# An attention phase on one core: one head's weighing moved behind a bank's copy, and the next weights split behind the exponentials and packings

## The chip, the core and the metric

The kernel runs on one core of a Trainium2 chip. The metric is the device time of one execution in microseconds. Five engines of the core matter here, each with its own list of instructions: TensorE (PE in the profile, its weight loads PEld) multiplies matrices into banks of PSUM, VectorE (DVE) and ScalarE (ACT) do the arithmetic around it, GpSimd (POOL) copies a little and issues some transfers, and SyncE's queue (SP) issues the other transfers between memory and SBUF.

## The reference, cut to what matters

The whole is a two-layer model on 512 tokens of width 1024: dilated attention, a feed-forward block, an mLSTM block, a feed-forward block and a last normalization. The change lies in the attention:

```python
proj = (xn @ w_in).reshape(B, S, N_GROUPS, 3, ATTN_HEADS, ATTN_HEAD_DIM)
for g, (window, dilation) in enumerate(((128, 1), (512, 4), (2048, 16))):
    q = apply_partial_rope(proj[:, :, g, 0], positions) * scale
    k = apply_partial_rope(proj[:, :, g, 1], positions)
    v = proj[:, :, g, 2]
    o, lse = dilated_window_attention(q, k, v, window, dilation)
wts = softmax(stack(lses), axis=0)
o = einsum('gbsh,gbshd->bshd', wts, stack(outs))
return o.reshape(B, S, ATTN_WIDTH) @ w_out
```

So there are three groups, and for each of 8 heads of size 128 a query, a key and a value in each group. The first 32 of 128 features of queries and keys are rotated. The softmax weights of the three groups are joined into one weighing of all probabilities.

## The kernel before, in words

**Split products.** Every float32 product is made of three products of rounded numbers. A weight chunk of 128 x 1024 is loaded raw, ScalarE casts it to the high half (L223, `whi`), and VectorE subtracts that from the raw chunk for the low half (L225, `wlo`). `split_chunk` does both. There are three raw buffers and four pairs of halves, so a chunk can be split only when the matmuls of the fourth chunk before it are done, and a raw buffer is free for its next load when its split is done.

**Pairs and groups.** Heads are taken in four pairs, `a0` to `a3` in the profile's names, and for each pair the three groups one after another (`project_pair`). For pairs 1 to 3 the first group is plain: queries (`a2g0q`) and keys (`a2g0k`) take two chunks each, with two PSUM banks each, and `evac` copies each bank out with a VectorE copy (L1001) and packs the rotated features with ScalarE (L1004). The second and third group (`a2g1`, `a2g2`; `qk_unit`) form queries and keys together by a scheme of seven block products, in the order P1, P5, P6, P2, P7, P3, P4, of 24 matmuls each. Their sums of weight blocks are VectorE subtractions (`less`, L880). P1 and P2 go to bank c, P5 and P3 to bank p, P6, P7 and P4 to bank u, which starts as a copy of c (L944). Three banks tagged `acc` serve the plain groups and these. After P2 and P4 the queries are taken out by ScalarE: the rotated features are packed (L906) and the bank copied (L924). After P7 and P3 VectorE adds a kept copy (L932) and ScalarE packs (L906). After P4 comes the rotation (`rope`): a shuffle (L607), two multiplications (L608, L609), an addition (L616), and four ScalarE copies back (L628). In the very last unit the rotation is done in parts, straight into place (L613).

**Attention of a pair.** `scores0` multiplies queries and keys of the first group, and VectorE adds the mask and takes the maximum (L709); `exponentials` turns the maximum into a shift (L747) and ScalarE takes eight exponentials (L752). `scores12` does the same for the other two groups (L733 on TensorE, L736, L757). `joint` exchanges maxima and sums between the groups (one small product on TensorE, L769) and forms the factors (L785 to L793). `weigh(i)` multiplies the probabilities of head i with them: four VectorE instructions at L801 and four at L804. `transposes(i)` turns the result (L810) and stores it to memory (L813), `bring(i)` loads it back in another order (L818), and `values(i)` multiplies with the values (L828, L833); the result is kept by a ScalarE copy (L640).

**The order of the work.** The attention of a pair runs spread over the projections of the next one. `defer(n, fn)` puts a function on a list for n ticks later; `advance` raises the tick after each chunk of the first group and after the second, fourth, sixth and seventh product of the other two, and calls what is due. Ticks 1 to 4 of a pair are its first group, 5 to 8 the second, 9 to 12 the third. `RUN_AT` says when each step of the pair before is due: `scores12` at 1, the list `rest` at (4, 5, 7, 8, 8, 9), `values` at 11 and 12. `project` calls what is due at tick 4 a little early, between the two banks of the last key chunk (`amid`). `SCORES0_AT` puts a pair's own `scores0` at tick 10, after P2 of its third group. A planner then makes the list of each engine out of the traced instructions; it may move an instruction ahead of others where nothing forbids it. `tc.issue_after(ins)` forbids it: what is traced under it comes behind `ins` on the engine of `ins`. `behind(fn, engine=E)` calls `fn` so behind the last instruction traced on E; `run` does it for TensorE. Two variables do it for the splits: the subtractions come behind `ahead_of_splits[0]` on VectorE, the casts behind `ahead_of_casts[0]` on ScalarE.

**Splits ahead.** `Feed` holds the plan of all weight chunks. `pop` hands out the next and tops the store up to `ahead`; after each product but a unit's first it is topped up to `ahead + 1`. From pair 1 on `ahead` is 3.

Of the kernel before, what the change touches and what calls it, by code (L numbers as in the profile page):

```python
# [33 lines left out]
C2 = float(np.float32(np.uint32(np.float32(TWO_PI - C1).view(np.uint32) & 0xFFFFF000).view(np.float32)))  # L34
C3 = float(np.float32(TWO_PI - C1 - C2))
SCORES0_AT = 6
RUN_AT = (1, (4, 5, 7, 8, 8, 9), (11, 12), (2, 3, 1))
LAST_AT = (1, (2,), (), (1, 1, 1))
STACK_AT = (9, 11, 15, 17)
HEAD_AT = ((9, 10, 12), (10, 11, 13), (12, 13, 15), (13, 14, 16), (15, 16, 18), (16, 17, 19), (18, 19, 21),  # L40
# [33 lines left out]
def tile_hybrid_dilated_attn_mlstm(  # L74
# [62 lines left out]
    tick = [0]  # L137
# [4 lines left out]

    def advance():
        tick[0] += 1
        run_deferred(lambda t: t <= tick[0])

    def run_deferred(due=lambda t: True):
        while True:
            ready = sorted((e for e in later if due(e[0])), key=lambda e: e[:2])
            if not ready:  # L150
                return
            later.remove(ready[0])
            ready[0][2]()
# [4 lines left out]
    def last_on(engine):  # L158
        for ins in reversed(nc.cur_bb.bb.instructions):
            if ins.engine == engine:  # L160
                return ins
# [43 lines left out]
    ahead_of_splits = [None]  # L205
# [198 lines left out]
    with ExitStack() as actx:  # L404
# [253 lines left out]
        def attention_pair(pr, qks):  # L658
# [35 lines left out]
            def scores0(q, k):  # L694

                for i in range(2):
                    for b2 in range(2):
                        sp = score_bank(i, "%ss0" % nm)
                        o, parts = 0, []
                        for b in (2 * b2, 2 * b2 + 1):  # L700
                            lo_ = max(b - 1, 0) * P
                            w = (b + 1) * P - lo_
                            nc.tensor.matmul(sp[:, o:o + w], q[:, i, b * P:(b + 1) * P],
                                             k[:, i, lo_:lo_ + w], start=True, stop=True)
                            parts.append((b, o, w))
                            o += w
                        for b, o, w in parts:
                            pb = max(2 * b - 1, 0)
                            nc.vector.tensor_tensor_reduce(  # L709
                                p0[i][:, pb:pb + w // P, :].rearrange("p a b -> p (a b)"),  # L710
                                sp[:, o:o + w], mask_band[:, 2 * P - w:], 1.0, -3e38,
                                op0=ALU.add, op1=ALU.max, accum_out=own[:, 0, 0, i, b:b + 1])
                ahead_of_splits[0] = last_on(DVE)

                def exps():
                    for i in range(2):
                        exponentials(0, i)
                if pr < HEADS // 2 - 1:
                    exps()
                else:  # L720
                    defer(2, lambda: behind(exps, engine=ACT))

# [73 lines left out]
            def weigh(i):  # L796
                cf4 = weight[0]
                for b in range(4):
                    pb = max(2 * b - 1, 0)
                    blk = p0[i][:, pb:2 * b + 1, :].rearrange("p a b -> p (a b)")  # L800
                    nc.vector.tensor_scalar(blk, blk, cf4[:, 0, i, b:b + 1], None, op0=ALU.mult)  # L801
                for c in range(4):
                    blk = p12[i].rearrange("p (g c) k -> p c g k", g=2)[:, c]
                    nc.vector.tensor_scalar(blk, blk, cf4[:, 1, i, c:c + 1], None, op0=ALU.mult)  # L804
# [11 lines left out]
            def bring(i, queue=nc.gpsimd):  # L816
                pt = ap2.tile([P, 4, 15, R], F32, tag="p", name=nm + "pT", bufs=4)
                queue.dma_start(pt.rearrange("p a n i -> p (a n i)"), pts[i].rearrange("b j a x -> (b j) (a x)"))  # L818
                pts[i] = pt
# [18 lines left out]
                else:  # L838
                    out(2 * pr + i, op)

            def first_rest():
                joint()
                weigh(0)
            rest = (first_rest, lambda: transposes(0), lambda: bring(0), lambda: weigh(1), lambda: transposes(1),
                    lambda: bring(1))
            if pr == HEADS // 2 - 1:
                def all_rest():
                    first_rest()
                    ahead_of_splits[0] = last_on(DVE)
                    ahead_of_casts[0] = last_on(ACT)  # L850
                    transposes(0)
                rest = (all_rest,)
# [44 lines left out]
        def qk_unit(pr, g, qk):  # L897
            nm = "a%dg%d" % (pr, g)
            last = pr == HEADS // 2 - 1 and g == 2
            target = {"P1": "c11", "P2": "c11", "P5": "p5", "P3": "p5", "P6": "u", "P7": "u", "P4": "u"}  # L900
            two_m = lambda t: t.rearrange("p (m s) -> p m s", m=2)
            acc = {}
            rot = vu = None

            def pack(q, src):
                nc.scalar.activation(two_m(rot[0][quarter(q)]), src, AF.Copy)  # L906

            def finish(name):
                nonlocal rot, vu
                if name == "P5":  # L910
                    vu = ap.tile([P, 2, SEQ], F32, tag="vu", name=nm + "vu")
                    nc.scalar.activation(vu[:, 0], acc["p5"], AF.Copy)
                    ahead_of_casts[0] = last_on(ACT)
                elif name == "P6":
                    nc.scalar.activation(vu[:, 1], acc["u"], AF.Copy)
                    ahead_of_casts[0] = last_on(ACT)
                elif name in ("P2", "P4"):
                    th = int(name == "P4")
                    src = two_m(acc[target[name]])
                    if th == 0:  # L920
                        t = ap.tile([P, 2, SEQ], F32, tag="rot", name="rot")
                        rot = t[:, 0], t[:, 1]
                    pack(th, src[:R])
                    nc.scalar.activation(halves(qk[0], th), src, AF.Copy)  # L924
                    ahead_of_casts[0] = last_on(ACT)
                    if last and th:
                        rope(qk, rot, False, 1, 2, True)
                elif name in ("P7", "P3"):
                    th = int(name == "P7")
                    out = halves(qk[1], th)  # L930
                    with behind_scores():
                        nc.vector.tensor_tensor(out, two_m(acc[target[name]]), two_m(vu[:, 1 - th]), op=ALU.add)  # L932
                    pack(2 + th, out[:R])
                    if last and th == 0:
                        rope(qk, rot, False, 0, 1, True)
                        rope(qk, rot, False, 2, 4, True)

            for n, name in enumerate(QK_ORDER):
                key = target[name]
                if name in ("P1", "P5"):  # L940
                    acc[key] = acc_tile(nm + key)
                if name == "P5":
                    acc["u"] = acc_tile(nm + "u")
                    nc.scalar.activation(acc["u"], acc["c11"], AF.Copy)  # L944
                    ahead_of_casts[0] = last_on(ACT)
                    feed.fill(feed.ahead + 1)
                whl = feed.pop()
                with fenced():
                    for m in range(2):
                        for k in range(4):  # L950
                            for a, b in SPLITS:
                                if name in ("P1", "P2", "P4"):
                                    x_ = pair[b][k + 4 * (name != "P1")][:, HALF * (name == "P4"):HALF * (1 + (name == "P4"))]
                                else:
                                    x_ = sum_part(name, b, k)
                                nc.tensor.matmul(acc[key][:, m * HALF:(m + 1) * HALF], whl[a][:, k, m * P:(m + 1) * P], x_,
                                                 start=(name in ("P1", "P5") and m == 0 and k == 0 and (a, b) == SPLITS[0]),
                                                 stop=(m == 1 and k == 3 and (a, b) == SPLITS[-1]), skip_group_check=True)
                finish(name)
                if n == 6 and not last:  # L960
                    back = rope(qk, rot, False)
                    if g == 2:
                        back()
                    else:
                        defer(1, lambda: behind(back, engine=ACT))
                if n in (1, 3, 5, 6):
                    advance()
                if n:
                    feed.fill(feed.ahead + 1)

        def project_pair(pr, qks, then=None):
            nm = "a%d" % pr
# [1411 lines left out]
```

## Time and profile before

| | us |
|---|---|
| median of 3 runs | 1394.45 |
| lowest and highest | 1393.76, 1394.7 |
| the profiled execution | 1396.64 |
| its span, first to last instruction | 1394.9 |
| TensorE busy | 1371.6 |
| VectorE busy | 1111.5 |
| ScalarE busy | 779.8 |

The profile is one execution. A row of a timeline begins with the start in us from the span's start and the duration in us; then come engine, line, operation, what is written and what is read (numbers of buffers left out), shape and count; in brackets stand the idle time before it and what ended that. A row of the list of waits gives who waited for whom, then the total in us, how often, and the longest. A row of the table by stage gives the stretch, its length, the busy us of PE, PEld, DVE, ACT and POOL, and last the granted clock of TensorE (1.00 is full), the busy share of the DMA engines and GB/s.

### The profile page before, as it was taken

What the parts mean: (1) busy time and instruction counts of PE and PEld (TensorE: products, weight loads), DVE (VectorE), ACT (ScalarE), POOL (GpSimd) and SP (SyncE); (2) the same over time, 40 slices, a digit from 0 to 9 for tenths busy, and PEclk for the clock granted to TensorE, in tenths of its full rate; (3) what the DMA queues carried; (4) which work ended last, traced back from release to release, by engine and by line L of the source; (5) the groups of instructions that cost most, each with busy time, mean ns of one, the idle gap of its engine ahead of it and who ended that gap; (6) DMA issues with size and microseconds to landing.
All of it is one profiled execution on the core that took longest, in us unless ns stands there. A gap on an engine that the chain in (4) does not pass through costs nothing. (4 is left out here: it accounts for less than half of the span.)

```text
span 1394.9 us, 22560 instructions
## 1 busy us (share of the span) xinstructions
PE 1371.6 (98%) x8740; PEld 1245.1 (89%) x8740; DVE 1111.5 (80%) x1845; ACT 779.8 (56%) x1246; POOL 178.7 (13%) x264
## 2 busy tenths in 40 slices
PE   9999999999999999999999999999999999999997
PEld 7888889898897889999999998897888899999886
DVE  7758769595878289877878898898858988887887
ACT  6556565655555245444567464785535554458854
POOL 3000013122211000000010100123201230001213
PEclk9999999999999999999999999999999999999999
DMA  8534245537275447333352743324334553335963
GB/s 288 183 121 137 81 146 182 174 117 230 81 252 168 150 138 169 102 121 121 106 154 74 172 118 92 91 76 118 95 116 112 145 181 122 122 110 131 198 165 100
DMA packets 140067, 193.81 MB, mean 139 GB/s; under 512 B 8980, under 2 KB 104788, under 8 KB 139960
## 3 DMA queue, kind: packets, MB, share of 16 engines
q1 hardware_dynamic: 119552, 139.81, 31.5%
q0 software_dynamic: 18752, 51.43, 15.6%
q8 instruction: 69, 1.13, 0.3%
q10 hardware_dynamic: 1656, 1.12, 0.2%
q14 instruction: 38, 0.31, 0.1%
HBM read 167.30 MB, written 22.54 MB: 136 GB/s over the span
## 5 line engine op out<-in xcount | busy, mean ns | idle before, releaser
L1687 POOL DMA_DIRECT2D f1T<-in_ffn_w_out_dram x15 | 17.8, 1185 | 208.7 <-DMA f1P_2w_w<-in_ffn_w_out_dram 136.2
L1662 POOL DMA_DIRECT2D f0S<-in_ffn_w_out_dram x10 | 8.7, 874 | 260.7 <-DVE f0hid L1579 173.0
L2219 POOL DMA_DIRECT2D hD<-hB x32 | 21.7, 696 | 68.5 <-DVE hB L2216 68.5
L255 PE MATMUL mo<-n_h,mo_k_l 128*128 128x512 f32 x64 | 25.3, 395 | 0.0
L255 PE MATMUL mo<-n_h,mo_k_h 128*128 128x512 f32 x64 | 25.2, 393 | 0.0
L255 PE MATMUL mo<-n_l,mo_k_h 128*128 128x512 f32 x64 | 25.2, 393 | 0.0
L255 PE MATMUL awo<-ao_h,awo_k_h 128*128 128x512 f32 x64 | 25.2, 393 | 0.0
L255 PE MATMUL mwo<-yo_l,mwo_k_h 128*128 128x512 f32 x64 | 25.1, 393 | 0.0
L255 PE MATMUL mqk<-n_h,mqk_k_h 128*128 128x512 f32 x64 | 25.1, 392 | 0.0
L255 PE MATMUL mqk<-n_l,mqk_k_h 128*128 128x512 f32 x64 | 25.1, 391 | 0.0
L255 PE MATMUL f0j<-n_h,f0j_h 128*128 128x512 f32 x64 | 25.0, 391 | 0.0
L255 PE MATMUL f1j<-n_h,f1j_h 128*128 128x512 f32 x64 | 25.0, 391 | 0.0
L255 PE MATMUL awo<-ao_h,awo_k_l 128*128 128x512 f32 x64 | 25.0, 391 | 0.0
L255 PE MATMUL mwo<-yo_h,mwo_k_l 128*128 128x512 f32 x64 | 25.0, 391 | 0.0
L255 PE MATMUL mqk<-n_h,mqk_k_l 128*128 128x512 f32 x64 | 25.0, 390 | 0.0
L255 PE MATMUL awo<-ao_l,awo_k_h 128*128 128x512 f32 x64 | 25.0, 390 | 0.0
L255 PE MATMUL f1j<-n_h,f1j_l 128*128 128x512 f32 x64 | 24.9, 390 | 0.0
L255 PE MATMUL f0j<-n_h,f0j_l 128*128 128x512 f32 x64 | 24.9, 390 | 0.0
L255 PE MATMUL f0j<-n_l,f0j_h 128*128 128x512 f32 x64 | 24.9, 389 | 0.0
L255 PE MATMUL f1j<-n_l,f1j_h 128*128 128x512 f32 x64 | 24.9, 389 | 0.0
L255 PE MATMUL mwo<-yo_h,mwo_k_h 128*128 128x512 f32 x64 | 24.8, 391 | 0.0
L225 DVE TENSOR_TENSOR v1P_l<-v1W,v1P_h 128x1024 fp32r<-128x1024 f32 x14 | 17.1, 1223 | 9.3 <-ACT v1P_h L223 9.3
(2613 smaller groups left out, 5881.1 us busy)
## 6 DMA issues: line engine op xcount, KB each, us to landing
f0j_w<-in_ffn_w_in_dram SPq DMA_DIRECT2D x17, 512.0 KB, 4.7
f1j_w<-in_ffn_w_in_dram SPq DMA_DIRECT2D x17, 512.0 KB, 6.5
f1T<-in_ffn_w_out_dram POOLq DMA_DIRECT2D x15, 512.0 KB, 7.0
f0hid<-in_ffn_w_in_dram SPq DMA_DIRECT2D x9, 512.0 KB, 6.4
f1hid<-in_ffn_w_in_dram SPq DMA_DIRECT2D x9, 512.0 KB, 4.9
v0W<-in_attn_w_in_dram SPq DMA_DIRECT2D x8, 512.0 KB, 6.8
v1W<-in_attn_w_in_dram SPq DMA_DIRECT2D x8, 512.0 KB, 3.6
awo_k_w<-in_attn_w_out_dram SPq DMA_DIRECT2D x8, 512.0 KB, 6.6
```

Source lines behind the costliest of these rows:

```text
L225: nc.vector.tensor_tensor(lo[:, :n], raw[:, :n], hi[:, :n].bitcast(F32), op=ALU.subtract)
L255: nc.tensor.matmul(acc, whl[a][:, k, m * P:(m + 1) * P], pairs[b][kk], start=(kk == 0 and (a, b) == SPLITS[0]), stop=(kk == nk - 1 and (a, ...
L1662: nc.gpsimd.dma_start(t, src[1][:, ks], accum_op=ALU.add)
L1687: nc.gpsimd.dma_start(view(to), weight_rows(hk * UNITS + u, n), accum_op=ALU.add)
L2219: nc.gpsimd.dma_start(hD[k // 4].rearrange("(b i) x -> i b x", i=R)[:, :, c0:c0 + R], t[R * a_:R * (a_ + 1)])
```

## The change

In pairs 1 to 3 the first entry of `rest`, which was `joint` and `weigh(0)` in one, becomes two. `joint` stays at tick 4. `weigh(0)` gets time 4.5: `advance` now calls all that lies under the next whole tick, so it is called when the tick becomes 4, after both key banks are traced, and behind the last VectorE instruction, which is the copy of the last key bank. In the third group the marks `ahead_of_splits` and `ahead_of_casts` are moved on: in pairs 1 and 2 behind the exponentials of `scores0`, then (all three pairs) behind P7's and P3's addition and packing, then in pairs 1 and 2 behind the rotation's copies; in the last unit `ahead_of_splits` goes behind the rotation after P4. And from P6 of the third group to its end `feed.ahead` is 2, so that P4's weights are split after `scores0` is traced and each chunk after that one product later. For the attention of pair 3 itself (`all_rest`) `joint` and `weigh(0)` stay together.

```diff
-RUN_AT = (1, (4, 5, 7, 8, 8, 9), (11, 12), (2, 3, 1))
+RUN_AT = (1, (4, 4.5, 5, 7, 8, 8, 9), (11, 12), (2, 3, 1))
...
     def advance():
         tick[0] += 1
-        run_deferred(lambda t: t <= tick[0])
+        run_deferred(lambda t: t < tick[0] + 1)
...
                 if pr < HEADS // 2 - 1:
                     exps()
+                    ahead_of_splits[0], ahead_of_casts[0] = last_on(DVE), last_on(ACT)
                 else:
                     defer(2, lambda: behind(exps, engine=ACT))
...
-            def first_rest():
-                joint()
-                weigh(0)
-            rest = (first_rest, lambda: transposes(0), lambda: bring(0), lambda: weigh(1), lambda: transposes(1),
+            rest = (joint, lambda: behind(weigh, 0, engine=DVE), lambda: transposes(0), lambda: bring(0), lambda: weigh(1), lambda: transposes(1),
                     lambda: bring(1))
             if pr == HEADS // 2 - 1:
                 def all_rest():
-                    first_rest()
+                    joint()
+                    weigh(0)
...
                         nc.vector.tensor_tensor(out, two_m(acc[target[name]]), two_m(vu[:, 1 - th]), op=ALU.add)
+                    if g == 2:
+                        ahead_of_splits[0] = last_on(DVE)
                     pack(2 + th, out[:R])
+                    if g == 2:
+                        ahead_of_casts[0] = last_on(ACT)
                     if last and th == 0:
...
                 finish(name)
+                if g == 2 and n == 2:
+                    feed.ahead = 2
+                if n == 6 and last:
+                    ahead_of_splits[0] = last_on(DVE)
                 if n == 6 and not last:
                     back = rope(qk, rot, False)
                     if g == 2:
                         back()
+                        ahead_of_splits[0], ahead_of_casts[0] = last_on(DVE), last_on(ACT)
                     else:
                         defer(1, lambda: behind(back, engine=ACT))
                 if n in (1, 3, 5, 6):
                     advance()
                 if n:
                     feed.fill(feed.ahead + 1)
+            feed.ahead = 3
```

## The prediction, made before the changed kernel ran

> **What bounds the kernel now.** The page of the profile comes first, for the share of each engine; then the list of waits of TensorE over the whole span, longest first, for where its idle time lies; then busy time by stage, for who is full there.
>
> ```profile
> span 1394.9 us, 22560 instructions
> PE 1371.6 (98%) x8740; PEld 1245.1 (89%) x8740; DVE 1111.5 (80%) x1845; ACT 779.8 (56%) x1246; POOL 178.7 (13%) x264
> ```
> ```profile
> PE a3s L733 <- DVE a3g_q L613: 2.6, 1, 2.6
> PE a2g1p L956 <- DVE a2g_k L1001: 2.0, 1, 2.0
> PE a3g1p L956 <- DVE a3g_k L1001: 2.0, 1, 2.0
> PE a1s L733 <- ACT a1g_k L628: 1.5, 1, 1.5
> ...
> PE a2s L733 <- ACT a2g_k L628: 1.5, 1, 1.5
> ```
> ```profile
> 284.00:320.00 36.00, 33.80 (x272) 33.16 (x272) 35.62 (x59) 22.08 (x32) 9.78 (x17) 1.00 0.48 146
> ...
> 320.00:340.00 20.00, 20.00 (x154) 19.18 (x154) 8.03 (x21) 10.77 (x25) 2.23 (x4) 1.00 0.70 239
> ```
>
> TensorE is busy for 98% of the span, so an edit that adds or removes no matmul can win only idle time, 23.3 us in all. The five waits quoted, 2.6 + 2.0 + 2.0 + 1.5 + 1.5 = 9.6 us, lie in the attention of pairs 1 to 3, and each names one of the orders that the diff rewrites: the copy of the last key bank (L1001), the turned keys copied back (L628), the turned queries of the last pair (L613). The stage rows (columns: stretch, length, PE, PEld, DVE, ACT) say what has to be watched: from the second group to the middle of the third VectorE is full, 35.62 of 36 us, and after that it has slack, 8.03 of 20.
>
> **Part 1, the weighing behind the last key bank.** VectorE in order of time (start, duration), first at pair 1, then at pair 2; then TensorE at pair 2.
>
> ```profile
> 205.65 0.69 DVE L1001 COPY a1g_k<-a1g0k 128x512 f32<-128x512 f32 x1
> ...
> 211.11 1.07 DVE L801 TENSOR_SCALAR a0p<-a0p,a0cf 128x128 f32<-128x128 f32 x4
> ...
> 285.21 1.07 DVE L801 TENSOR_SCALAR a1p<-a1p,a1cf 128x128 f32<-128x128 f32 x4
> 286.20 1.13 DVE L804 TENSOR_SCALAR a1p<-a1p,a1cf 128x256 f32<-128x256 f32 x4
> 287.25 0.68 DVE L1001 COPY a2g_k<-a2g0k 128x512 f32<-128x512 f32 x1
> 287.85 1.21 DVE L225 TENSOR_TENSOR a2g1P_l<-a2g1W,a2g1P_h 128x1024 fp32r<-128x1024 f32 x1
> ...
> 313.25 2.31 DVE L225 TENSOR_TENSOR a2g2P_l<-a2g2W,a2g2P_h 128x1024 fp32r<-128x1024 f32 x2
> ```
> ```profile
> 285.75 0.28 PE L956 MATMUL a2g1c<-xa_h,a2g1P_l 128*128 128x256 f32 x1
> 288.08 0.47 PE L956 MATMUL a2g1p<-S,a2g1P_h 128*128 128x256 f32 x2 [2.05 <-DVE a2g_k L1001]
> ...
> 314.49 0.39 PE L956 MATMUL a2g2c<-xa_h,a2g2P_l 128*128 128x256 f32 x1 [0.15 <-DVE a2g2P_l L225]
> ```
>
> P1 of the second group ends at 285.75 + 0.28 = 286.03, and P5 needs the bank that the copy empties. Eight multiplications (four L801, four L804) stand ahead of it, 287.25 - 285.21 = 2.04 us. Behind the copy instead, it ends about 285.21 + 0.68 = 285.9 and P5 starts 2.05 us earlier; pair 3 has the same row at 2.0. In pair 1 the copy already stands ahead of the weighing (205.65 against 211.11), so nothing is won there.
>
> What is late next: VectorE's work is the same, only reordered. The low half of P2's weights in the third group ends about 313.25 + 1.2 = 314.4 and already stops TensorE for 0.15 us. If TensorE alone came 2.05 us earlier, it would wait 2.2 us there, and part 1 would be worth nothing. It pays only if VectorE's full stretch also starts earlier, which part 2 decides.
>
> **Part 2, exponentials and packings ahead of the casts.** First ScalarE, then VectorE, then TensorE at the end of pair 2's third group.
>
> ```profile
> 331.22 1.06 ACT L223 ACTIVATE a3g0k_k_h<-a3g0k_k_w 128x1024 fp32r<-128x1024 f32 x1 [2.79 <-DMA a3g0k_k_w<-in_attn_w_in_dram]
> 332.19 0.39 ACT L752 ACTIVATE a2p<-a2p,a2nb 128x128 f32<-128x128 f32 x1
> ...
> 335.42 0.50 ACT L752 ACTIVATE a2p<-a2p,a2nb 128x256 f32<-128x256 f32 x1
> ...
> 337.96 0.59 ACT L906 ACTIVATE rot<-a2g2u 32x512 f32<-32x512 f32 x1
> ...
> 342.49 1.27 ACT L628 ACTIVATE a2g_q<-rot 32x512 f32<-32x512 f32 x2 [1.88 <-DVE rot L616]
> 343.77 1.28 ACT L628 ACTIVATE a2g_k<-rot 32x512 f32<-32x512 f32 x2
> ```
> ```profile
> 322.10 0.29 DVE L709 CUSTOM_DVE_ANT_0 a2p<-a2s,acst 128x128 f32<-128x128 f32 x1 [1.81 <-DMA a1pD<-a1pB]
> ...
> 323.35 0.17 DVE L747 TENSOR_SCALAR a2nb<-a2own 128x4 f32<-128x4 f32 x1
> ...
> 338.59 0.73 DVE L607 STREAM_SHUFFLE rot<-rot 128x512 f32<-128x512 f32 x1
> ...
> 339.97 0.69 DVE L609 TENSOR_TENSOR rot<-rot,sinn 128x512 f32<-128x512 f32 x1
> ```
> ```profile
> 329.56 0.28 PE L956 MATMUL a2g2u<-xa_h,a2g2P_l 128*128 128x256 f32 x1
> ...
> 332.19 1.05 PE L828 MATMUL a1o<-a1pT,a1v 128*128 128x128 f32 x8
> ...
> 344.45 2.26 PE L733 MATMUL a2s<-a2g_k,a2g_q 128*128 128x128 f32 x16 [1.48 <-ACT a2g_k L628]
> ```
>
> The exponentials could start when the shift is ready, 323.35 + 0.17 = 323.5; they start at 332.19, behind casts of the next pair's weights that wait for DMA, and ScalarE takes nothing out of turn here. They take 335.42 + 0.6 - 332.19 = 3.8 us, and the packings and the rotation queue up behind them, so that the keys are back only at 345.05.
>
> In the new order they run from about 323.6 to 327.4. P4's last packing then follows P4's end (332.19) at once: packing 0.59, shuffle 0.73, three passes of 0.69 (cosine and addition taken like the sine row), four copies back 1.27 + 1.28, together 5.9 us: keys back at 338.1, or 338.7 with one other copy in between. The scores want them at 344.45 - 1.48 = 342.97, so this wait goes, with 4 us to spare: 1.5 us at pair 1 and 1.5 us at pair 2. It comes back only if that chain grows by those 4 us.
>
> The price is P4's own weights, which are now split behind the exponentials: 327.4 + 1.06 for the cast + 1.21 for the subtraction (the row of P2) = 329.7, and P4 needs the low half at 329.56. That is a wait of 0.1 us if nothing else gets in between, none if the masks' wait of 1.81 us for a store shrinks, and 1.4 us if two packings of 0.6 come first. I take 0.3 us in each of pairs 1 and 2, nearest to the row, so 0.6; ends 0 and 2.8.
>
> ScalarE and VectorE then reach the next pair's second group earlier: copies back end at 338.7 instead of 345.05, and the scores are not held up, so masks, exponentials and first subtractions of that group start 4 to 6 us sooner. They are held again by the weight buffers, which are freed by matmuls, so I let VectorE's full stretch start 3 us earlier by the clock. That is about as much as TensorE gains up to there (1.5 + 2.05 - 0.3), so P2 in the third group waits a little more than today: 0.4 us each in pairs 2 and 3, 0.8 in all; ends 0 and 4.1 (part 1 refunded).
>
> **Part 3, one split less ahead.** Loads follow the splits, because a split frees the raw buffer. The first key load of the next pair starts after P4's split, 329.7, instead of about 319.5.
>
> ```profile
> 319.45 6.59 SPq L201 DMA_DIRECT2D a3g0k_k_w<-in_attn_w_in_dram  x2
> ...
> 352.13 0.39 PE L255 MATMUL a3g0k<-xa_h,a3g0k_k_h 128*128 128x512 f32 x1
> ```
> ```profile
> a3g0k_k_w<-in_attn_w_in_dram SPq DMA_DIRECT2D x2, 512.0 KB, 9.3
> ```
>
> With 9.3 us to land, 1.06 for the cast and 1.21 for the subtraction it is ready at 341.3; the first key matmul is at 352.13. The query matmuls and scores cover it: nothing, and without that cover at most the 10.2 us shift itself.
>
> **Part 4, the last pair.** ScalarE, then VectorE.
>
> ```profile
> 414.75 0.63 ACT L906 ACTIVATE rot<-a3g_k 32x512 f32<-32x512 f32 x1
> ...
> 416.68 0.59 ACT L906 ACTIVATE rot<-a3g2u 32x512 f32<-32x512 f32 x1
> ...
> 423.83 0.68 DVE L613 TENSOR_TENSOR a3g_q<-rot 32x512 f32<-32x512 f32 x1
> ```
>
> The packings of P7, P3 and P4 all stand behind value casts that wait for DMA, and the last queries are finished only at 423.83 + 0.68. Now P7's and P3's packings and the keys' rotation come before P4 ends; what is left after P4's own packing is a shuffle and three passes, 2.8 us, far ahead of the scores: 2.6 us won, lower end 0 (a value cast that still waits for DMA ahead of the packing).
>
> **Sum.** 9.6 - 0.6 - 0.8 = 8.2 us. One term I leave out. The half clock after pair 3's wait:
>
> ```profile
> 368.30:372.00 3.70, 3.67 (x18) 3.70 (x19) 3.70 (x6) 2.28 (x4) 0.00 (x0) 0.54 0.00 0
> ...
> 288.00:291.70 3.70, 3.62 (x30) 3.65 (x31) 3.70 (x6) 2.82 (x5) 0.00 (x0) 1.00 0.02 4
> ```
>
> After the 2.0 us gap the granted clock (third column from the right) is 0.54 for 3.7 us, 1.7 us lost; after pair 2's gap of 2.05 us it stays 1.00. So the loss is an accident of one execution, and I don't count it against the median. The Trainium skill (TensorE: Matmul & The Clock Gate, "The HAM clock gate") lets the clock fall after an idle window of about 3.4 us that runs freely; by that page neither gap is long enough and no loss was due, and this trace disagrees at one gap and agrees at the other. By the page the sum is 8.2 us, by pair 3's row 9.9.
>
> The profiled execution took 1396.64 us, 2.2 above the median of 1394.45, and the 1.7 us of half clock may be most of that. From the profiled one: 1396.64 - 8.2 - 1.7 = 1386.7. From the median: 1394.45 - 8.2 = **1386.2**.
>
> **The rivals.**
>
> *VectorE takes part 1 back.* Its full stretch starts no earlier, and P2 of the third group waits 2 us more in pairs 2 and 3. For it: the 35.62 of 36. Against it: the 8.03 of 20, slack that the earlier exponentials let VectorE use. 9.6 - 4.0 - 0.6 = 5.0: 1389.4 us.
>
> *The clock loss is in the usual execution too* and goes with its gap: 8.2 + 1.7 = 9.9: 1384.5 us. For it, pair 3; against it, pair 2.
>
> *It does only half of what it says.* Part 1 is refunded, and in the last pair a value cast that waits for DMA still stands ahead of P4's packing, so that 2.6 stays: 3.0 - 0.6 = 2.4: 1392.0 us.
>
> *Slower: P4's weights are late.* Place: P4 in the third group of pairs 1 and 2. All that stands ahead of its split hangs on the masks' second half, which waits for a store to land (the 1.81 row). Each us by which the exponentials end after 327.4 is paid twice. From 4.4 us on the 8.8 us of the other terms are gone, from 5.8 it is slower by over 0.2%; at 7 us it is 1394.45 - 8.8 + 14 = 1399.7 us. Against it: the landing would have to come at 327 or later; for it: a planner sets the order on ScalarE, and packings or kept outputs may stand ahead too.
>
> **How the numbers follow.** Chances: forecast 0.40, VectorE takes it back 0.20, clock 0.14, half 0.10, slower 0.16. A measurement of this kernel can tell about 0.2%, 2.8 us. The first three are faster by more, 0.74; half is within, 0.10; slower 0.16. The range runs from 1394.45 - 9.6 - 1.7 = 1383.1, no price paid, to 1392.5, which takes in the half case's own time.
>
> **What would show it.** Right: no wait at a1s, a2s, a2g1p, a3g1p, a3s; exponentials (L752) near 327 at pair 2 and ahead of all casts of pair 3's weights; L1001 ahead of L801. Wrong: waits of 1 us or more at a2g2u or a1g2u (P4) or at a2g2c and a3g2c (P2), on L225, or a wait at the key matmuls on a load.

## The result, and the profile after

The changed kernel takes 1385.12 us, the median of 4 runs (1384.77 to 1386.5). The kernel before took 1394.11 beside it (1393.17 to 1394.7). The ratio is 0.9938, with a 95% interval of 0.9921 to 0.9955: 9.0 us faster. The profiled execution took 1385.26 us.

The page of the profile first, after the change:

```profile
span 1383.5 us, 22546 instructions
PE 1368.5 (99%) x8740; PEld 1242.9 (90%) x8740; DVE 1111.3 (80%) x1845; ACT 780.5 (56%) x1246; POOL 180.2 (13%) x264
```

VectorE and ScalarE are as busy as before to 0.7 us: only the order is another. TensorE's idle time falls from 23.3 to 15.0 us. Its busy time falls by 3.1 us with the same 8740 matmuls; 1.7 of that is the stretch at half clock, which this execution doesn't have. Next TensorE's list of waits, longest first:

```profile
PE idle L108 <- DVE idle_w L103: 1.5, 1, 1.5
...
PE a2g2p L959 <- ACT a2g_q L923: 0.3, 1, 0.3
...
PE a1g2u L959 <- DVE a1g2P_l L225: 0.2, 1, 0.2
```

All five quoted waits are gone, and the longest that is left stands at the program's start. In the attention two small ones are new, at P5 of pair 2's third group (0.31 us, at 304.89) and at P4 of pair 1 (0.24). The profile's lines are shifted by up to 9: 752 is now 753, 906 is 905, 1001 is 1010. ScalarE at the end of pair 2's third group, in order of time:

```profile
318.01 0.40 ACT L753 ACTIVATE a2p<-a2p,a2nb 128x128 f32<-128x128 f32 x1 [2.81 <-DVE a2nb L748]
...
321.26 0.49 ACT L753 ACTIVATE a2p<-a2p,a2nb 128x256 f32<-128x256 f32 x1
...
321.75 1.04 ACT L223 ACTIVATE a2g2P_h<-a2g2W 128x1024 fp32r<-128x1024 f32 x1
...
329.04 0.59 ACT L905 ACTIVATE rot<-a2g2u 32x512 f32<-32x512 f32 x1 [1.32 <-PE a2g2u L959]
...
333.83 1.28 ACT L628 ACTIVATE a2g_k<-rot 32x512 f32<-32x512 f32 x2
```

The exponentials wait for nothing but their shift (a2nb), P4's packing for nothing but P4's matmuls. The keys are back at 335.11, where it was 345.05. TensorE, around the old gaps and at P2 (the last two rows are the scores of pair 2 and pair 3):

```profile
249.69 0.39 PE L959 MATMUL a1g2u<-xa_h,a1g2P_l 128*128 128x256 f32 x1 [0.24 <-DVE a1g2P_l L225]
...
284.37 0.40 PE L959 MATMUL a2g1p<-S,a2g1P_h 128*128 128x256 f32 x2
...
310.74 0.28 PE L959 MATMUL a2g2c<-xa_h,a2g2P_h 128*128 128x256 f32 x1
310.86 0.28 PE L959 MATMUL a2g2c<-xa_l,a2g2P_h 128*128 128x256 f32 x1
311.15 0.39 PE L959 MATMUL a2g2c<-xa_h,a2g2P_l 128*128 128x256 f32 x1
...
337.67 3.74 PE L734 MATMUL a2s<-a2g_k,a2g_q 128*128 128x128 f32 x32
...
412.89 1.95 PE L734 MATMUL a3s<-a3g_k,a3g_q 128*128 128x128 f32 x16
```

Of these rows only P4 of pair 1 has a bracket, 0.24 us: the price that the prediction put at 0.3. VectorE at pair 2's second and third group:

```profile
277.94 1.23 DVE L225 TENSOR_TENSOR a2g1P_l<-a2g1W,a2g1P_h 128x1024 fp32r<-128x1024 f32 x1 [1.21 <-ACT a2g1P_h L223]
...
282.36 0.68 DVE L1010 COPY a2g_k<-a2g0k 128x512 f32<-128x512 f32 x1
282.96 1.07 DVE L802 TENSOR_SCALAR a1p<-a1p,a1cf 128x128 f32<-128x128 f32 x4
...
309.89 2.34 DVE L225 TENSOR_TENSOR a2g2P_l<-a2g2W,a2g2P_h 128x1024 fp32r<-128x1024 f32 x2
```

The copy stands ahead of the weighing (L802, then L805) and ends at 283.04, 1.3 us before P5 wants its bank. In before the subtraction of 277.94 stood at 281.00. By stage, with the columns as before:

```profile
281.00:317.00 36.00, 35.68 (x284) 34.84 (x284) 35.11 (x62) 21.44 (x31) 10.67 (x18) 1.00 0.51 154
317.00:337.00 20.00, 20.00 (x155) 19.15 (x154) 8.97 (x19) 14.22 (x31) 4.05 (x8) 1.00 0.74 237
```

VectorE is as full as it was, 35.11 of 36. TensorE is now full beside it (35.68, where it had 33.80): VectorE's work lies earlier, it hasn't become less.

### The profile page after: what moved, and what is told of

Same layout as the page of the kernel before. It is cut to its first block, busy times and chain, and to the rows that moved or that the text cites. A ratio compares the mean times of both kernels' runs of the same rounds, so it can differ in the third digit from the quotient of the medians.

```text
span 1383.5 us, 22546 instructions
## 1 busy us (share of the span) xinstructions
PE 1368.5 (99%) x8740; PEld 1242.9 (90%) x8740; DVE 1111.3 (80%) x1845; ACT 780.5 (56%) x1246; POOL 180.2 (13%) x264
```

## The experiments

**Theory.** The waits at a1s, a2s, a2g1p and a3g1p have one cause, the exponentials that start late behind casts; a3s has a cause of its own, the value casts of the last pair. **Rival:** each wait hangs on the edit that names it, as the prediction's four terms have it. Each kernel was timed in turn with the kernel before, on one chip; the medians of before were 1394.75, 1394.53 and 1394.6 in the three sets. The numbers are those of the labels; there is no seventh.

**1. Part 1 alone.** The kernel before with the diff's edits to `RUN_AT`, `advance`, `rest` and `all_rest`, and none of the marks:

```diff
-            rest = (first_rest, lambda: transposes(0),
+            rest = (joint, lambda: behind(weigh, 0, engine=DVE), lambda: transposes(0),
```

> The kernel before with part 1 alone: the first head's weighing goes behind the copy of the last key bank, nothing else. Theory (VectorE takes it back): the waits at a2g1p and a3g1p go, a1s, a2s and a3s stay, and P2 of the third group (a2g2c, a3g2c) waits about 2 us more on L225, since VectorE is full up to there; time within 0.5 us of before, about 1394. Rival (the parts add up): no new wait at P2, time 4.0 us below before, about 1390.

Measured: 1392.11 us, ratio 0.998 (0.9971 to 0.9989). TensorE's waits in its profile:

```profile
PE a1s L733 <- ACT a1g_k L628: 1.5, 1, 1.5
...
PE a3g1u L954 <- DVE a3g_k L930: 1.0, 1, 1.0
...
PE a2g2p L954 <- ACT a2g_q L922: 0.7, 1, 0.7
PE a3g2p L954 <- ACT a3g_q L922: 0.6, 1, 0.6
...
PE a2g1u L954 <- DVE a2g_k L930: 0.5, 1, 0.5
```

The two gaps at P5 shrink from 2.0 us to 0.2 and nothing, and 1.0 + 0.7 + 0.6 + 0.5 = 2.8 us of these 4.0 come back a few products later, where a bank is freed: 1.5 behind VectorE's additions and 1.3 behind ScalarE's copies, and none at P2, where the theory had put them. So most of what part 1 wins at P5 is taken back when nothing lets VectorE start earlier. Of the waits that were expected to stay, a1s did, but a2s and a3s are gone. At a2s the third cast ahead of the exponentials is done 2.4 us earlier (it starts at 328.82, in before at 331.22), and with it the keys are back at 342.65 and not at 345.05. At a3s the loads of the last pair came out in another order, which runs 8, 12 and 13 test. So most of the 2.6 us that part 1 wins by itself doesn't come from the gaps that it was made for.

**2. All but part 1.** The changed kernel with `joint` and `weigh(0)` in one again and the weighing at its old place.

> The changed kernel without part 1: weighing and exchange stay together ahead of the copy of the last key bank, all marks and the depth of two as changed. Theory A (fixed terms): a2g1p and a3g1p wait 2.0 us each as before, a1s, a2s and a3s are gone; 4.0 us above the changed kernel, about 1389. Theory B (VectorE comes 3.06 us earlier by the clock and TensorE only 1.5, as the two traces show): the copy ends 1.6 us earlier relative to TensorE, so each of the two waits is about 0.5 us; 1.0 us above the changed kernel, about 1386.

Measured: 1386.02 us (1385.21 to 1391.6), ratio 0.9938 (0.9924 to 0.9951). The old gap at P5 of pair 2, in TensorE's order of time:

```profile
285.96 0.47 PE L961 MATMUL a2g1p<-S,a2g1P_h 128*128 128x256 f32 x2 [0.50 <-DVE a2g_k L1012]
```

It is 0.50 us and not 2.05, and pair 3 has none, although the weighing stands ahead of the copy again. So the marks and the lesser depth take 1.5 us of this gap by themselves; on top of them part 1 is worth the 0.9 us between the medians, which the intervals don't tell from nothing. The profiled execution, 1391.6 us, is the slowest of the five: it has a wait of 2.0 us for the transfer of a3pT, of which run 10 shows 0.4 us and no other run as much, with a stretch at half clock behind it, and 0.9 us at a3s.

**3. Depth 3.** The changed kernel without `feed.ahead = 2`.

> The changed kernel with the depth of three kept in the third group. Theory: the depth of two only puts P4's split behind the exponentials; with three it is ahead of them, the wait of 0.24 us at P4 of pair 1 goes, nothing else changes: within 0.5 us of the changed kernel, about 1385. Rival: with three, casts of the next pair's queries that wait for DMA stand ahead of P7's and P3's packings again, the chain to the keys gets late, a1s and a2s wait up to 1.5 us each and a3s up to 2.6: up to 5 us above the changed kernel, about 1390.

Measured: 1385.37 us, ratio 0.9933 (0.9921 to 0.9946). The wait of 0.24 us at P4 of pair 1 goes, as expected; beside the other edits the depth does nothing that can be measured.

**4. The last pair as before.** The changed kernel with the marks behind P7, P3 and P4 and the lesser depth left out in pair 3:

```diff
-                    if g == 2:
+                    if g == 2 and not last:
                         ahead_of_splits[0] = last_on(DVE)
...
-                if n == 6 and last:
-                    ahead_of_splits[0] = last_on(DVE)
```

> The changed kernel, but in the third group of the last pair the marks behind P7's and P3's addition and packing, the mark behind the last rotation and the depth of two are left away. Theory: the packings of the last pair stand behind value casts that wait for DMA again and a3s waits 2 to 2.6 us; about 2.4 us above the changed kernel, 1387.5. Rival: with the earlier start the loads land in time and a3s does not wait in either form; within 0.5 us of the changed kernel.

Measured: 1385.82 us, ratio 0.9934 (0.9922 to 0.9947), and no wait at a3s. ScalarE in the last pair:

```profile
398.37 1.06 ACT L223 ACTIVATE a3g12v_k_h<-a3g12v_k_w 128x1024 fp32r<-128x1024 f32 x1 [5.81 <-DMA a3g12v_k_w<-in_attn_w_in_dram]
...
406.21 0.59 ACT L905 ACTIVATE rot<-a3g2u 32x512 f32<-32x512 f32 x1 [1.59 <-PE a3g2u L959]
```

The value casts stand ahead of the packings again, and yet P4's packing (406.21) waits for TensorE alone, since the values land in time: on SP's queue the load of the kept heads (oT) now goes first, at 388.01, and six value loads follow. In before two value loads went first, then oT, then four, and the third cast waited until 413.67. Here are SP's queue and that cast in before, then SP's queue in the changed kernel:

```profile
396.75 1.86 SPq L324 DMA_DIRECT2D a3g12v_k_w<-in_attn_w_in_dram  x2
398.79 1.46 SPq L647 DMA_DIRECT2D oT<-oD  x1
...
413.67 1.06 ACT L223 ACTIVATE a3g12v_k_h<-a3g12v_k_w 128x1024 fp32r<-128x1024 f32 x1 [0.17 <-DMA a3g12v_k_w<-in_attn_w_in_dram]
```
```profile
387.02 0.37 SPq L647 DMA_DIRECT2D oT<-oD  x1
```

So the marks are not needed against this wait when the loads come in this order. What turned the loads is part 1: in all six kernels that have it and leave the loads to the planner (the changed one and runs 1, 3, 4, 5 and 11) oT goes first, and in the four without it (before and runs 2, 6 and 10) it goes behind two value loads. Why the planner does so isn't shown. Runs 8 and 12 turn the loads by themselves, run 13 turns them back.

**5. Without the mark behind the exponentials.**

```diff
                     exps()
-                    ahead_of_splits[0], ahead_of_casts[0] = last_on(DVE), last_on(ACT)
```

> The changed kernel without the mark behind the exponentials of scores0 (pairs 1 and 2); the marks behind P7, P3 and the copies back stay, and so does the weighing's place. Theory: this mark carries part 2. Without it the casts of the next pair's weights stand ahead of the exponentials again and wait for their loads, the waits a1s and a2s come back at 1 to 1.5 us each and VectorE comes later, so that P2 or P5 of the next groups wait too: about 1388.5 us, 3 to 4 us above the changed kernel. Rival: the later marks (P7, P3, copies back) hold the casts back enough by themselves: within 0.7 us of the changed kernel's 1385.1.

Measured: 1385.32 us, ratio 0.9928 (0.9914 to 0.9941). The theory of this run fell: the mark that seemed to carry part 2 isn't needed beside the others.

**6. That mark alone.** The kernel before with this one line added.

> The kernel before with one line more: the mark behind the exponentials of scores0 in pairs 1 and 2. Theory: this mark alone takes away a1s and a2s and lets VectorE start its full stretch earlier, so that a2g1p and a3g1p shrink to 0.5 us or less although the weighing stands where it was: 1387 to 1389 us. a3s stays at 2.6 us if the order of the last loads stays as it was, and goes if that order changes. Rival: without the marks behind P7, P3 and the copies the casts only move to the places ahead of the packings, and a1s and a2s stay: 1393 to 1394.5 us.

Measured: 1387.21 us, ratio 0.9945 (0.9932 to 0.9957), 7.3 us of the 9. The top of TensorE's list of waits, then VectorE at the copy of pair 2's last key bank:

```profile
PE a3s L734 <- DVE a3g_q L613: 1.7, 1, 1.7
```
```profile
281.19 1.08 DVE L802 TENSOR_SCALAR a1p<-a1p,a1cf 128x128 f32<-128x128 f32 x4
282.18 1.14 DVE L805 TENSOR_SCALAR a1p<-a1p,a1cf 128x256 f32<-128x256 f32 x4
283.23 0.68 DVE L1002 COPY a2g_k<-a2g0k 128x512 f32<-128x512 f32 x1
```

The weighing stands ahead of the copy as in before, but all of it is 4.0 us earlier (285.21 there, 281.19 here), and P5 doesn't wait. One line takes four of the five waits away, two of them on VectorE's queue. It holds back both the casts on ScalarE and the subtractions on VectorE; no run has the two apart.

**10 and 11. Two other edits, each without that mark.** The tenth adds only the lesser depth to the kernel before. The eleventh is the changed kernel without the mark behind the exponentials and without the lesser depth: the marks behind P7, P3, P4 and the copies back are left, and part 1.

> The kernel before with one thing more: feed.ahead is 2 from P6 of the third group to its end (pairs 1 to 3), and none of the new marks. Theory: this depth and the mark behind the exponentials are substitutes, since the casts that stood ahead of the exponentials are those of chunks three and four ahead: a1s and a2s shrink to 0.5 us or less, VectorE comes earlier, a2g1p and a3g1p shrink; a3s stays, since the last loads keep their order (two value loads, oT, the rest): 1387 to 1390 us. Rival: depth does nothing, with the marks or without: 1394 to 1395 us.

> The changed kernel without the mark behind the exponentials and without the lesser depth; the marks behind P7, P3, the copies back and in the last pair stay, and so does the weighing's place. Theory of substitutes: with both covers gone the casts of the next pair's keys stand ahead of the exponentials again, a1s and a2s come back at 1 to 1.5 us each: 1387.5 to 1390 us. Rival: the marks behind P7, P3 and the copies are enough by themselves: within 0.8 us of the changed kernel's 1385.1.

Measured: 1386.78 us, ratio 0.9947 (0.9933 to 0.9961), and 1385.7 us, ratio 0.9936 (0.9923 to 0.9948). ScalarE up to the first exponential of pair 2, with the depth alone and then with the late marks:

```profile
318.95 1.06 ACT L223 ACTIVATE a3g0q_k_h<-a3g0q_k_w 128x1024 fp32r<-128x1024 f32 x1 [3.71 <-DMA a3g0q_k_w<-in_attn_w_in_dram]
322.35 1.06 ACT L223 ACTIVATE a3g0q_k_h<-a3g0q_k_w 128x1024 fp32r<-128x1024 f32 x1 [2.34 <-DMA a3g0q_k_w<-in_attn_w_in_dram]
323.31 0.38 ACT L752 ACTIVATE a2p<-a2p,a2nb 128x128 f32<-128x128 f32 x1
```
```profile
319.56 1.06 ACT L223 ACTIVATE a3g0q_k_h<-a3g0q_k_w 128x1024 fp32r<-128x1024 f32 x1 [3.73 <-DMA a3g0q_k_w<-in_attn_w_in_dram]
320.53 0.39 ACT L752 ACTIVATE a2p<-a2p,a2nb 128x128 f32<-128x128 f32 x1
```

Before the change three casts stood ahead of the exponentials, and the third, of the next pair's first key chunk, waited until 331.22. With the depth two are left, with the late marks one, with the first mark none; the exponentials start at 323.31, 320.53 and 318.57, against 332.19. In all three the four waits are 0.2 us or less. The number of casts ahead hardly matters; what matters is how long the last of them waits for its load, as run 1 suggests too, where all three are still ahead. The eleventh run's theory, that depth and first mark stand in for each other and nothing else does, fell: the late marks are a third stand-in. (Run 11 has part 1 too, which bears on two of the four waits.) The tenth run missed in one point: a3s was expected to stay, and it is gone, although the loads have their old order and the last pair has no marks. With the lesser depth only two value casts stand ahead of the packings, and P4's packing starts at 404.59. Its median is 1.7 us above the changed kernel's and its profiled execution, 1385.08, the fastest of the five, so what the slower ones have left isn't seen.

**8. The loads turned by themselves.** The kernel before, with oT's load ahead of all value loads on SP's queue:

```diff
+                if n == 2 and last:
+                    bring_heads(slice(0, 4))
+                    ahead_of_loads[0] = last_on(mybir.EngineType.SP)
...
+            with tc.issue_after(ahead_of_loads[0]) if ahead_of_loads[0] is not None else nullcontext():
+                nc.sync.dma_start(raw.rearrange("p (k g n) -> p k g n", k=2, n=w)[:, :, i],
+                                  part[2 * ch * P:2 * (ch + 1) * P].rearrange("(k p) n -> p k n", p=P))
```

> The kernel before with the load order of the last pair changed by itself: the load of the kept heads (oT) goes first on SP's queue and the last value chunks' loads (a3g12v) queue behind it, as the changed kernel has them. Theory: the 2.6 us at a3s came from value loads that stood behind the 1 MB of oT, so that the value casts ahead of the packings waited until 412 us; with the order turned a3s shrinks to 0.5 us or less and the time falls by about 2.5 us, to 1391.5 to 1392.2. Rival: the wait hangs on the order on ScalarE (casts ahead of packings) whatever the loads do: a3s stays above 2 us and the time is 1394 to 1394.7.

Measured: 1393.49 us, ratio 0.9991 (0.9983 to 1.0). The wait at a3s falls from 2.6 to 0.2 us, so the mechanism holds; the 1.0 us between the medians is less than half of the 2.5 expected, and its upper end is 2.4. Where the rest went isn't settled. Run 9 shows that in another execution of before this wait is 1.6 us and not 2.6.

**12. The mark of run 6 and the loads of run 8.**

> The kernel before with the mark behind the exponentials (pairs 1 and 2) and with the last pair's loads turned (oT first, the value loads behind it); no other mark, weighing where it was. Theory: the mark alone left one wait, a3s at 1.7 us, and that hangs on the loads: it goes, and the time is 1385 to 1386 us, the changed kernel's. Rival: the wait moves on to what follows (a value cast or the first value matmuls): 1386.8 to 1387.6 us, as with the mark alone.

Measured: 1385.23 us, ratio 0.9934 (0.9921 to 0.9946). The wait at a3s falls from 1.7 to 0.2 us, and these two edits give the changed kernel's time without any of its other edits.

**13. The changed kernel with the loads in their old order.** oT's load queues behind the first value chunk's two:

```diff
+                with tc.issue_after(first_loads[0]):
+                    nc.sync.dma_start(t[:, ks], oD[ks].rearrange("k p s -> p k s"))
```

> The changed kernel with the last loads in the order of before: oT's load is queued behind the first value chunk's two, the other value loads behind oT. All marks stay. Theory: the load order alone decides a3s, so the wait comes back at 1.5 to 2.6 us and the time is 1386.5 to 1388 us. Rival: the marks of the last pair do what they were predicted to do, they let the packings pass late value casts: no wait at a3s, and within 0.7 us of the changed kernel's 1385.1.

Measured: 1385.37 us, ratio 0.9938 (0.9925 to 0.995), no wait at a3s. SP's queue, then ScalarE:

```profile
388.35 2.52 SPq L325 DMA_DIRECT2D a3g12v_k_w<-in_attn_w_in_dram  x2
391.05 0.43 SPq L651 DMA_DIRECT2D oT<-oD  x1
391.58 1.33 SPq L325 DMA_DIRECT2D a3g12v_k_w<-in_attn_w_in_dram  x2
```
```profile
397.93 0.63 ACT L909 ACTIVATE rot<-a3g_k 32x512 f32<-32x512 f32 x1 [5.55 <-DVE a3g_k L935]
398.58 1.06 ACT L224 ACTIVATE a3g12v_k_h<-a3g12v_k_w 128x1024 fp32r<-128x1024 f32 x1
...
405.14 0.59 ACT L909 ACTIVATE rot<-a3g2u 32x512 f32<-32x512 f32 x1 [1.29 <-PE a3g2u L963]
```

The packings now pass the value casts (397.93 ahead of 398.58), as part 4 said. So marks and load order each take the wait away: with both as in before but the first mark it is 1.7 us (run 6), with the loads turned 0.2 (run 12), with the marks none (run 13), with both none (the changed kernel). Run 2 has the marks and the old order as well, and there 0.9 us are left at a3s, not behind the queries but behind a kept output (`o_keep`) that stands behind a waiting value cast. The theory that the loads alone decide fell.

**9. The kernel before, profiled once more.**

> The kernel before, unchanged, profiled once more. Theory: the half granted clock of 3.7 us after pair 3's 2.0 us gap was an accident of one execution: the rows show it at another place or not at all. Rival: it follows that gap in every execution, and the granted clock is about 0.54 behind a3g1p's wait again.

Measured: 1396.54 us. The longest of the old waits in its list, and two stretches by stage:

```profile
PE a3g1p L956 <- DVE a3g_k L1001: 2.0, 1, 2.0
PE a1s L733 <- ACT a1g_k L628: 1.7, 1, 1.7
PE a3s L733 <- DVE a3g_q L613: 1.6, 1, 1.6
...
PE a2s L733 <- ACT a2g_k L628: 1.4, 1, 1.4
...
PE a2g1p L956 <- DVE a2g_k L1001: 0.4, 1, 0.4
```
```profile
265.80:269.50 3.70, 3.70 (x15) 3.17 (x14) 3.34 (x23) 0.33 (x1) 0.00 (x0) 0.54 1.03 255
...
368.30:372.00 3.70, 3.44 (x16) 3.47 (x17) 3.70 (x7) 2.37 (x4) 0.00 (x0) 0.54 0.00 0
```

The half clock is back behind a3g1p's gap, and a second one stands behind a1s. TensorE loses 1.7 us by that one, and its wait at a2g1p falls from 2.05 to 0.42: P5 starts at 288.34, where it was 288.08. Of these 0.26 us, 0.25 were there ahead of the lost clock (a1s starts at 264.45, in before at 264.20). There VectorE set the time, and the lost clock cost next to nothing. So a row of the list of waits tells what TensorE has left to lose at that place, not what is won when it goes.

## Why the prediction was right, point by point

**The time** was forecast at 1386.2 us and measured at 1385.12: the waits that were to go went, and the prices were smaller than taken. On the profiled executions 9.6 us of waits went and 0.31 + 0.24 = 0.55 are new, 9.05 against the forecast's 8.2. Of the span's 11.4 us that leaves 2.35: 1.7 are the half clock, and 0.65 I can't place. So it wasn't only idle time that could be won: TensorE's busy time fell too. The total held and the shares of the parts did not, as the next points show; that is in part luck.

**Part 2** was right, and larger than its term. The exponentials ran from 318.0 to 321.8 and not to 327.4, since the whole pair came earlier: P2 of the third group starts at 310.74 against 313.94. The keys are back 3.0 us before the forecast. VectorE's full stretch started 3.06 us earlier by the clock (277.94 against 281.00), where 3 was taken.

**Part 1** is the term that was mis-sized. The prediction gave it 2.05 + 2.0 less 0.8 and tied it to VectorE's earlier start. The condition was right (run 1, without it, gives 2.8 us back) and the rows said more than was read from them: a VectorE that is 3 us earlier brings the copy 3 us earlier as well, so most of the gap goes without any reordering. Runs 2 and 6 show it: 0.50 us left in the one, none in the other. What part 1 does besides, turning the last pair's loads, was not foreseen. The sum came out because each wait was counted once, whichever part took it.

**The prices.** P4's was put at 0.6 in two pairs and is 0.24 in pair 1 and nothing in pair 2. P2's was to grow by 0.8 and shrank in pair 2: the low half holds the matmul of 311.15 by 0.17 us (at the step of 0.12 it was due at 310.98), where by the same count it was 0.31 (314.49 against 314.18). In pair 3 no wait of 0.2 us or more stands there. The slower rival's place was P4, and its point of 4.4 us was never near.

**Part 3** was right in what it cost, nothing (run 3). That the lesser depth could by itself do nearly the whole work (run 10) was not seen.

**Part 4** was right in its mechanism (run 13) and not needed for it: with part 1 the planner also put oT's load first, which is enough by itself (runs 4, 12). The prediction read the casts on ScalarE and not the order of the loads on SP's queue that made them late.

**The clock** was the step that failed: the loss was put at nothing. It was called an accident of one execution on the strength of one gap that kept its clock. The second execution shows it at the same place and at one more; the mean granted clock is 0.9971 over 39 executions of before and 0.9984 over 49 of the ten kernels that keep at most one of the five waits above 1 us: 0.0012 of 1390 us, some 1.7 us. These means also hold the last 3 to 6 us of each execution, where TensorE has run out of work and its clock is at half. That costs 2.9 us of clock in both traces of before and 2.4 in the mean of the ten others, so 1.2 to 1.7 us are left, or somewhat under one such stretch per execution. So the second rival, 1384.5 us, was right that the loss comes back, and the time lies between its figure and the forecast's. How much of the loss was paid is not settled, since run 9 shows one that cost next to nothing.

No run beats the changed kernel: its time is reached by several (runs 3, 5, 12, 13), all within 0.3 us.

## What to carry to other kernels

Before waits are added up as separate terms, look for the one instruction far upstream that makes several of them late: here, in each pair, a cast that waited for its load stood ahead of the exponentials and held them (in pair 2 by 8.7 us, 332.19 against a shift that was ready at 323.5), and four waits of TensorE hung on it, two by way of ScalarE and two by way of VectorE. Where several edits each remove that one cause they don't add; the test is each alone, not only each left out, since every leave-one-out run here shows nothing. And where a planner orders the queues, compare the order of the loads too, for an edit to one engine's order can move them as well: here the weighing's new place turned the last pair's loads.

## What the runs showed of the hardware

The granted clock falls to half for 3.41 us behind some gaps of TensorE of about 2 us and not behind others. (The 0.54 over 3.7 us in the rows is 0.50 over 3.41: in windows of 0.1 us the clock of before is 1.00 up to 368.46, 0.50 from 368.47 to 371.87 and 1.00 again from 371.88.) Run 8's stage rows at both places:

```profile
289.30:293.00 3.70, 3.70 (x21) 3.70 (x19) 3.70 (x5) 1.54 (x2) 0.00 (x0) 0.54 0.26 62
...
368.00:372.00 4.00, 3.22 (x27) 3.25 (x28) 4.00 (x7) 2.48 (x5) 0.00 (x0) 1.00 0.00 0
```

It is the same pair of gaps as in before with the two outcomes exchanged. The fourteen traces show what decides: the clock changes only at the ends of fixed slots of 3.413 us. The two falls of run 9, at 266.05 and 368.45, are 102.40 us apart, 30 such slots. If each trace's slots are laid out from its own falls (where it has no other, from the one at its end, when TensorE has run out of work), the eleven longest gaps ahead of that end sort by the idle time within one slot:

| gap | idle in one slot, us | clock at the slot's end |
|---|---|---|
| a2g1p 2.03, run 8 | 2.03 | falls |
| a3o 2.01, run 2 | 2.01 | falls |
| a3g1p 1.99, before | 1.99 | falls |
| a3g1p 2.01, run 9 | 1.90 | falls |
| a1s 1.74, run 9 | 1.74 | falls |
| a3s 1.70, run 6 | 1.70 | stays |
| a1s 1.59, run 8 | 1.59 | stays |
| a3s 2.62, before | 1.58, and 1.04 in the next | stays |
| a2g1p 2.05, before | 1.54, and 0.51 in the slot ahead | stays |
| a3g1p 1.98, run 8 | 1.08, and 0.91 in the next | stays |
| a3s 1.64, run 9 | 0.85, and 0.78 in the next | stays |

So a gap costs the clock when more than about half a slot of it, between 1.70 and 1.74 us, falls into one slot. A gap of 2 us that a slot's end cuts near its middle keeps the clock, and where the slots lie differs from execution to execution. That is why pair 2's gap paid nothing in before and paid in run 8. The slots have the length of the free-running idle window of about 3.4 us that the Trainium skill gives (TensorE: Matmul & The Clock Gate, "The HAM clock gate"); but a whole idle window, as stated there, wasn't needed for any of these five falls, all behind shorter gaps.
